# Cutting the first half of the tokens into two blocks of 512 columns instead of three, with the split inputs of both halves in one tile, spread side work and a later norm

## The chip, the cores and the metric

The kernel runs on one core of one Trainium2 chip. TensorE (PE) multiplies, VectorE (DVE), ScalarE (ACT) and GpSimd (POOL) do the elementwise work, and SyncE (SP) issues the DMAs. The metric is the device time of one execution in microseconds. Before the change three runs took 2689.2, 2690.6 and 2692.82 us; the median is 2690.6 us.

## What is computed

The reference is one inference step of one layer over 2048 prompt tokens and 64 sample tokens (8 sequences of 8), with 1024 model columns:

```python
mod = einsum('bd,de->be', silu(c), w_ada) + b_ada
sh1, sc1, g1, sh2, sc2, g2 = split(mod, 6)
h = rmsnorm(x, norm_mix_w) * (1 + sc1) + sh1
proj = einsum('bld,de->ble', h, w_in)
o_dn  = gated_deltanet(silu(conv4(qkv)), z, b, a)   # q, k normalised per head; 4 heads of 128
o_swa = sliding_window_attention(sq, sk, sv)        # 8 q heads, 2 kv heads, window 128
x = x + g1 * einsum('ble,ed->bld', concat(o_dn, o_swa), w_out)
h = rmsnorm(x, norm_ffn_w) * (1 + sc2) + sh2
gate, up = split(conv3(einsum('bld,df->blf', h, w_up)) + conv_b, 2)
x = x + g2 * einsum('blf,fd->bld', silu(gate) * up, w_down)
y = rmsnorm(x, final_norm_w)
```

The output also holds the new states of the convolutions, of the DeltaNet and of the attention cache. The arithmetic is float32.

## The kernel before

**Products.** Activations lie with the model columns on the partitions and the tokens along the free dimension. A projection is worked out one output row group of 128 columns (m) and one block of tokens (bi) at a time. Weights and inputs are split into a high and a low part that the faster float32 matmul takes, and each product is made of three: high by high, high by low and low by high (`gemm_steps`, L319). So one m on one block takes 8 (k) times 3 matmuls, all into one PSUM bank. The input projection has 22 m, the output projection 8, the up projection 44.

**Halves and blocks.** The tokens are cut into two halves, and each half into three blocks: `HALVES = [[(0, 384), (384, 384), (768, 256)], [(1024, 384), (1408, 384), (1792, 320)]]` (L36). The second half's up projection is mostly done with a cheaper scheme of its own (`up_quarters`), and the down projection has its own blocks of 512; neither is touched, apart from one norm.

**Order of the work.** Python generators lay the work out. `beside(steps, filler, share)` (L334) takes one step of side work and then so many steps (three matmuls each) of a projection as filler; `rest` runs what is left of the filler. `lockstep` runs several generators a step at a time in turn, `chain` one after the other. The framework then orders the instructions of each engine by that order and its own timing estimates, so an instruction can stand somewhat earlier on its engine than the Python text says; each engine runs its own list in order. All DMAs are issued by SP.

The stages, with their times in the profile:

1. 0 to 82 us: the inputs and the first modulation weights (w_ada, comps 0 and 1) are loaded; as each of eight k of the modulation comes, `affine_h` makes the split input h of the blocks for that k and the first two m of the input projection take it (`first_two`, steered by `PLAN`).
2. 82 to about 262 us: m 2 to 11 of the first half as filler beside the tasks: the rest of the modulation (`ada_cols`), the sums of down weights (`weight_sums`), the bias tables, the gates and the norm of the second half's tokens (`x_rstd`). `SHARE[3]` = 8.
3. 262 to 360 us: m 12 to 21 beside the first chunks of the DeltaNet (`ahead`).
4. 360 to 820 us: the second half's input projection beside the DeltaNet and attention of the first half (`mixers`). When the first half's h block is read for the last time, `freed` calls `second`, which makes the second half's h in the place.
5. 820 to 950 us: `between(0)`: the output projection of the first half (`outproj`, weights by `out_weights`), its norm and the next h (`ffn_in`).
6. 917 to 1612 us: the first half's up projection, beside the second half's mixers and the sample work (950 to 1478 us); then `between(1)`, the second half's up projection in two schemes (to 2206 us), and the down projection in two passes of seven products with the last norm (`down_phase`).

**Evacuation.** `conv_block` (L515) takes a PSUM bank: ACT copies it into a buffer and starts the convolution, DVE adds the other taps, three in the input projection and two in the up projection (L531). `silu2` (L542) makes twice the SiLU out of a Tanh (ACT, L545) and one more DVE instruction (L546); the factor two is taken out later, in `front`.

**Where h lies.** Each block has its own high and low tile, `hi0`, `lo0`, `hi1` and so on, and its own tile for the factors of the norm (`sg0`, `sg1`, `sg2`).

Of the kernel before, what the change touches and what calls it, by code (L numbers as in the profile page):

```python
# [14 lines left out]
F32 = mybir.dt.float32  # L15
# [7 lines left out]
P = 128  # L23
D = 1024
KT = 8
# [10 lines left out]
HALVES = [[(0, 384), (384, 384), (768, 256)], [(1024, 384), (1408, 384), (1792, 320)]]  # L36
# [58 lines left out]
def kernel(  # L95
# [69 lines left out]
    def ada_load(comp, kt, wpool, wt=None):  # L165
        if wt is None:
            wt = wpool.tile([P, KT, P], F32, tag="wada", name="wada", bufs=4)
        loads.append(nc.sync.dma_start(wt, I["w_ada"][KT * comp + kt]).ins)
        return wt
# [99 lines left out]
    def x_rstd(hf, bi, rB, pool, bank):  # L269

        c0, n = HALVES[hf][bi]
        acc = pool.tile([P, HB[0]], F32, tag="xacc", name="xacc", bufs=2)[:, :n]
        for k in range(KT):
            x = pool.tile([P, HB[0]], F32, tag="xst", name="xst", bufs=5)[:, :n]
# [7 lines left out]
        yield from token_rstd([acc], n, rB, pool, bank)  # L282

    def first_rstd(bi, xs, rB, pool, bank, eng):
# [3 lines left out]
        for k in range(KT):  # L288
            t = pool.tile([P, HB[0]], F32, tag="xst", name="xst", bufs=XST)[:, :n]
# [11 lines left out]
    def rB_tile(bi):  # L301
        return gw.tile([P, HB[bi]], F32, tag=f"sg{bi}", name=f"rB{bi}")

# [53 lines left out]
    def project(ms, src, load, hb, hf, evac, after=None, freed=None, tags=("acc",), turn=(2, 2), third=None, w0=None):  # L357


        order = list(pairs(ms, turn))  # L360
# [5 lines left out]
        for i, (m, bi) in enumerate(order):  # L366
            ps = bank(src, tags[i % len(tags)])
            yield from gemm_steps(ps, w[m], hb[bi], HALVES[hf][bi][1])
            if bi == 2 and new:
                w[new[0]] = load(new[0])  # L370
                new.pop(0)
            evac(m, bi, ps)
            if bi == 2 and after:
                after(m)
# [7 lines left out]
    def pairs(ms, turn):  # L382
# [4 lines left out]
        for g in [ms[:a]] + [[m] for m in ms[a:b]] + [ms[b:]]:  # L387
            for bi in range(3):
                for m in g:
                    yield m, bi  # L390
# [124 lines left out]
    def conv_block(ps, n, np_, hist, state, w, bias, dst):  # L515
# [3 lines left out]
        rb = evp[0].tile([P, 3 + HB[0]], F32, tag="rb", name="rb", bufs=evp[1])  # L519
# [20 lines left out]
        return rb  # L540

# [29 lines left out]
    def in_evac(hf, bi, m, ps, ic):  # L571
# [20 lines left out]
    def inproj(hf, h, ic, ms, **kw):  # L592
        return project(ms, "in_ps", lambda m: load_split(I["w_inT"][m], nc.gpsimd if m % 2 else nc.vector), h, hf,
# [28 lines left out]
    def front(c, d, pool, rows=P):  # L622
# [17 lines left out]
        for i in range(2):  # L640
# [7 lines left out]
            yield True  # L648

        nc.vector.tensor_scalar_add(ss[:rows], ss[:rows], 4 * EPS)  # L650
# [16 lines left out]
        nc.vector.tensor_scalar_mul(nr[:rows, :, 0], nr[:rows, :, 0], 0.5)  # L667
# [461 lines left out]
    def mix_tiles(op):  # L1129
        return [[op.tile([P, KT, HB[bi]], F32R, tag=f"{t}{bi}", name=t) for t in ("mixh", "mixl")] for bi in range(3)]  # L1130

    def mix_load(hf, bi, mix, op):
        c0, n = HALVES[hf][bi]
        hi, lo = mix[bi]
        for k in range(KT):
            if bi < 2:
                tag, bufs = (("xr", 2), ("acc", 3))[k % 2]
                t = op.tile([P, HB[0]], F32, tag=tag, name="mt", bufs=bufs)[:, :n]
# [11 lines left out]
    def out_weights():  # L1150

        seq = [m for o in OUT_ORDER for m in o]
# [10 lines left out]
    def outproj(hf, bi, mix, sums, op, weights, kept=None):  # L1163
# [3 lines left out]
        if kept is not None:  # L1167
            x2 = op.tile([P, KT, HB[0]], F32, tag="mixh0", name="x2")
            kept += [[x2[:, m] for m in range(KT)], op.tile([P, KT, LS], F32, tag="mixl0", name="x2s")]
        sums[bi] = op.tile([P, HB[0]], F32, tag="acc", name="acc", bufs=3)  # L1170
        c0, n = HALVES[hf][bi]
        np_ = n - LS if c0 + n == LT else n
        for i, m in enumerate(OUT_ORDER[bi]):
# [3 lines left out]
            xr = kept[0][m] if kept else op.tile([P, HB[0]], F32, tag="xr", name="xr", bufs=2)  # L1177
# [18 lines left out]
    def between(hf, filler, es, ms):  # L1196
# [3 lines left out]
        mix, sums = mix_tiles(op), {}  # L1200
        beside(chain(mix_load(hf, 0, mix, op), mix_load(hf, 1, mix, op)), filler, SHARE[4])
        rest(filler)
        weights = out_weights()
        steps = outproj(hf, 0, mix, sums, op, weights)
        beside(mix_load(hf, 2, mix, op), steps, 2)
        rest(steps)
        h = [h_tile(bi) for bi in range(3)]
# [927 lines left out]
```

## Time and profile before

| what | value |
| --- | --- |
| median of three runs | 2690.6 us |
| the profiled execution: own time, span of its instructions | 2689.79 us, 2688.0 us |
| PE busy | 2606.4 us, 97% of the span |
| weight loads (PEld, beside PE) busy | 2403.3 us, 89% |
| DVE, ACT, POOL busy | 1899.5, 1305.9, 788.2 us |
| mean granted PE clock | 0.99 |
| DMA | 438.07 MB, 163 GB/s over the span |

A view by windows gives the busy time of each engine in a stretch of time, the granted clock of PE (1.00 is full) and the rate of the DMAs. A view of groups gives, for one line, engine, operation and shape, how many there were, their busy time in us and the mean of one in ns, and what ended the idle time before them. The timeline gives single instructions: start and length in us, and in brackets how long the engine idled before, and for whom. Matmuls overlap in the pipeline, so the length of one is longer than the time it adds; the distance between the starts of neighbours is what counts. PE busy at 97% is for the same reason not PE at its peak.

### The profile page before, as it was taken

Reading aid. Unit: us, or ns where it says so; the run is one execution under the profiler, and the core shown is the slowest. Engines: PE = TensorE matmul, PEld = TensorE weight load, DVE = VectorE, ACT = ScalarE, POOL = GpSimd, SP = SyncE. Lnnn points to the kernel's source line nnn. Section 1 sums busy time; section 2 is a strip of 40 time slices with the busy share of each in tenths; the row PEclk is TensorE's granted clock in tenths of the full one; section 3 lists DMA queues with packets and bytes.
Section 4 is the critical chain, followed back from the end, with each engine's and each line's share of the span. In section 5 each row is a group of like instructions: output and inputs, shape, how many; then the busy total and the mean of one; then the engine's idle time right before and its main releaser. Section 6 shows DMA issues by size and latency. Waiting matters only on the chain.

```text
span 2688.0 us, 50078 instructions
## 1 busy us (share of the span) xinstructions
PE 2606.4 (97%) x18344; PEld 2403.3 (89%) x18344; DVE 1899.5 (71%) x3933; ACT 1305.9 (49%) x3404; POOL 788.2 (29%) x682
## 2 busy tenths in 40 slices
PE   7998999999999999999999999999999999999998
PEld 5898988788999998888898899999999997879988
DVE  7667579888523778898868565786776666676676
ACT  6444255555233555455553454555555554444343
POOL 2024243343222412222211113345555520020022
PEclk9999989999999999999999999999999999999999
DMA  7677444232256542333245337324555458677673
GB/s 281 229 266 247 123 144 117 78 96 83 92 146 202 178 141 78 96 99 88 74 155 186 117 111 253 130 82 156 171 168 174 172 181 297 213 248 246 224 244 131
DMA packets 318660, 438.07 MB, mean 163 GB/s; under 512 B 83107, under 2 KB 221572, under 8 KB 318148
## 3 DMA queue, kind: packets, MB, share of 16 engines
q1 hardware_dynamic: 318412, 434.85, 49.6%
q8 instruction: 144, 2.36, 0.4%
q14 instruction: 104, 0.85, 0.1%
HBM read 320.44 MB, written 115.33 MB: 162 GB/s over the span
## 4 chain that ended last, share of the span: by engine, by line
PE 57%; DMA 5%; DVE 4%; issue 2%; POOL 2%; ACT 1%; SPq 0%; POOLq 0%; DVEq 0%; ACTq 0%
PE up_ps L324 20%; PE dn_ps L1751 13%; PE op_ps L324 5%; PE uq_b L1541 4%; PE uq_c L1541 2%; PE in_ps L324 2%; PE uq_g L1541 2%; PE uq_u L1541 2%; DMA tr<-T_d 1%; DMA rawu<-in_w_upT_dram 1%; PE uq_a L1541 1%; PE pv_ps L971 1%; DMA rawg<-in_w_upT_dram 1%; PE as_ps L934 1%; DVE w_lo L316 1%
## 5 line engine op out<-in xcount | busy, mean ns | idle before, releaser
L324 PE MATMUL up_ps<-hi,w_hi 128*128 128x384 f32 (+2 forms) x1152 | 377.0, 327 | 0.0
L324 PE MATMUL up_ps<-hi,w_lo 128*128 128x384 f32 (+2 forms) x1152 | 370.4, 322 | 0.6 <-DVE w_lo L316 0.6
L324 PE MATMUL up_ps<-lo,w_hi 128*128 128x384 f32 (+2 forms) x1152 | 370.7, 322 | 0.0
L324 PE MATMUL in_ps<-hi,w_hi 128*128 128x384 f32 (+2 forms) x1056 | 346.7, 333 | 3.8 <-ACT hi L265 1.1
L324 PE MATMUL in_ps<-lo,w_hi 128*128 128x384 f32 (+2 forms) x1056 | 347.6, 330 | 2.2 <-DVE lo L266 1.3
L324 PE MATMUL in_ps<-hi,w_lo 128*128 128x384 f32 (+2 forms) x1056 | 346.8, 329 | 1.3 <-POOL w_lo L316 1.3
L1751 PE MATMUL dn_ps<-th,wh 128*128 128x512 f32 (+2 forms) x796 | 273.1, 344 | 4.9 <-DVE x L1219 4.0
L1751 PE MATMUL dn_ps<-tl,wh 128*128 128x512 f32 (+2 forms) x796 | 273.2, 343 | 3.6 <-DVE tl L1643 3.6
L1751 PE MATMUL dn_ps<-th,wl 128*128 128x512 f32 (+2 forms) x796 | 272.3, 344 | 0.0
L324 PEld LDWEIGHTS up_ps<-hi,w_hi 128*128 128x128 f32 x1152 | 217.4, 189 | 15.9 <-issue 10.2
L324 PEld LDWEIGHTS up_ps<-lo,w_hi 128*128 128x128 f32 x1152 | 217.5, 189 | 8.6 <-issue 7.3
L324 PEld LDWEIGHTS up_ps<-hi,w_lo 128*128 128x128 f32 x1152 | 217.3, 189 | 8.7 <-issue 6.4
L324 PEld LDWEIGHTS in_ps<-hi,w_hi 128*128 128x128 f32 x1056 | 199.7, 190 | 18.2 <-issue 10.2
L324 PEld LDWEIGHTS in_ps<-lo,w_hi 128*128 128x128 f32 x1056 | 201.0, 190 | 11.0 <-issue 4.5
L324 PEld LDWEIGHTS in_ps<-hi,w_lo 128*128 128x128 f32 x1056 | 201.0, 190 | 8.3 <-issue 4.9
L316 DVE TENSOR_TENSOR w_lo<-w_raw,w_hi 128x1024 fp32r<-128x1024 f32 x111 | 140.7, 1268 | 83.2 <-ACT w_hi L315 82.2
L315 ACT CAST w_hi<-w_raw 128x1024 fp32r<-128x1024 f32 x132 | 138.0, 1046 | 119.6 <-PE in_ps L324 39.2
L531 DVE SCALAR_TENSOR_TENSOR ev<-rb,cw,ev 128x384 f32<-128x384 f32 (+1 forms) x216 | 147.3, 688 | 34.0 <-ACT ev L524 31.4
L1751 PEld LDWEIGHTS dn_ps<-th,wh 128*128 128x128 f32 x796 | 151.7, 191 | 21.9 <-ACT wh L1642 2.5
L1751 PEld LDWEIGHTS dn_ps<-tl,wh 128*128 128x128 f32 x796 | 151.6, 190 | 19.7 <-DVE tl L1643 3.9
L1751 PEld LDWEIGHTS dn_ps<-th,wl 128*128 128x128 f32 x796 | 151.4, 190 | 15.7
L1642 ACT CAST wh<-wr 128x512 fp32r<-128x512 f32 x149 | 92.1, 618 | 149.4 <-PE dn_ps L1751 119.6
(545 smaller groups left out, 6728.2 us busy)
## 6 DMA issues: line engine op xcount, KB each, us to landing
w_raw<-in_w_upT_dram SPq DMA_DIRECT2D x50, 512.0 KB
wada<-in_w_ada_dram SPq DMA_DIRECT2D x44, 512.0 KB
w_raw<-in_w_inT_dram SPq DMA_DIRECT2D x44, 512.0 KB
wr<-ws_d SPq DMA_DIRECT2D x88, 256.0 KB
w_raw<-in_w_outT_dram SPq DMA_DIRECT2D x40, 512.0 KB
proj<-ev SPq DMA_DIRECT2D x88, 192.0 KB
d<-act_d SPq DMA_DIRECT2D x33, 512.0 KB
wr<-in_w_downT_dram SPq DMA_DIRECT2D x66, 256.0 KB
```

Of the source, the lines that this page charges most:

```text
L315: nc.scalar.copy(hi, raw)
L316: (eng or nc.vector).tensor_tensor(lo, raw, hi.bitcast(F32), ALU.subtract)
L324: nc.tensor.matmul(ps[:, :n], a[:, k, :], b[:, k, :n], start=first is not False and k == ks[0] and i == 0, stop=last is not False and k == ...
L531: nc.vector.scalar_tensor_tensor(out, src(j), w[:, j:j + 1], out, ALU.mult, ALU.add)
L934: nc.tensor.matmul(banks[v][:, 256 * g + P * k0:256 * g + 256], a[r, g0 + g], b[r, keys], start=i == 0, stop=i == 2, tile_position=(64 * v ...
L971: nc.tensor.matmul(pv_ps[64 * v:64 * v + 64, :], (vprev[0], vt)[half][:, 64 * v:64 * v + 64], PT[v, half], start=half == k0, stop=half == 1)
L1541: nc.tensor.matmul(bk[t][:, :nb], u[:, k], v[:, k], start=new and k == 0 and y == 0, stop=k == KG - 1 and y == 2, skip_group_check=True)
L1642: nc.scalar.copy(h, raw)
L1751: nc.tensor.matmul(acc[m, s][:, :n], w[q, i][a][:, c], th[b][:, v], start=new and i == 0 and y == 0, stop=i == KH - 1 and y == 2, skip_gro ...
```

## The change

1. The first half has two blocks of 512. Loops over `range(3)` become loops over the number of blocks. The second half keeps its three.
2. One tile for the high and one for the low part (`h_at`), of 8 times 1088 columns; `h_tile(hf, bi)` gives a block's slice of it. The norm's factors (`sg_at`) likewise. A block of the second half no longer lies exactly where a block of the first half lay, so `second` makes h in two goes: block 0 and a quarter of block 1 when the first block is free, the rest when the second is.
3. In the first half's input projection SiLU is ACT's own function (`TWICE`), without the DVE instruction; DVE makes all low parts of weights there, where POOL made those of odd m.
4. Side work is spread: `spaced` adds empty steps, and the shares fall accordingly: `SHARE[3]` from 8 to 2.05, `SHARE[0]` from 8 to 5.4, `SHARE[2]` from 6 to 4, and others. At the start, `PLAN` is that of two blocks, the modulation weights have six buffers of their own (before: four, and four more in tiles of h), and the first load of x is 512 columns.
5. In the first pass of the down projection the norm of group 2 starts one product later (after j = 5 instead of j = 4), as it does in the second pass.

```diff
-HALVES = [[(0, 384), (384, 384), (768, 256)], [(1024, 384), (1408, 384), (1792, 320)]]
+HALVES = [[(0, 512), (512, 512)], [(1024, 384), (1408, 384), (1792, 320)]]
+NX = HALVES[1][0][1]
...
-    def h_tile(bi):
-        return [slot.tile([P, KT, HB[bi]], F32R, tag=f"{t}{bi}", name=f"{t}{bi}") for t in ("hi", "lo")]
+    h_at = []
+
+    def h_tile(hf, bi):
+
+        c0, n = HALVES[hf][bi]
+        a = KT * (c0 - HALVES[hf][0][0])
+        return [t[:, a:a + KT * n].rearrange("p (k n) -> p k n", k=KT) for t in h_at]
...
-        yield from token_rstd([acc], n, rB, pool, bank)
+        yield from spaced(token_rstd([acc], n, rB, pool, bank))
+
+    def spaced(steps, n=4):
+
+        for _ in steps:
+            for _ in range(n):
+                yield True
...
-            silu2(ev, rb)
+            if TWICE[hf] == 2:
+                silu2(ev, rb)
+            else:
+                nc.scalar.activation(ev, ev, AF.Silu)
...
-        return project(ms, "in_ps", lambda m: load_split(I["w_inT"][m], nc.gpsimd if m % 2 else nc.vector), h, hf,
+        return project(ms, "in_ps", lambda m: load_split(I["w_inT"][m], nc.gpsimd if hf and m % 2 else nc.vector), h, hf,
...
-        for bi in range(2):
-            steps = outproj(hf, bi + 1, mix, sums, op, weights, kept if bi else None)
+        for bi in range(nb - 1):
+            steps = outproj(hf, bi + 1, mix, sums, op, weights, kept if bi + 2 == nb else None)
             beside(ffn_in(hf, bi, h, sums, op), steps, SHARE[5])
             rest(steps)
         up = up_proj(hf, h, uc[0], op, ms)
-        beside(ffn_in(hf, 2, h, sums, op, *kept), up, SHARE[6])
+        beside(ffn_in(hf, nb - 1, h, sums, op, *kept), up, SHARE[6][hf])
...
-            if j == 4 and not ip:
-                finish = norm(2, 0, PW, x, sums[2], cols[2], free[4:6], wait=2)
-            elif j == 4:
+            if j == 4:
                 late = (2, 0, PW, x, sums[2], cols[2])
-            elif j == 5 and ip:
-                finish = norm(*late, free[-2:])
+            elif j == 5:
+                finish = norm(*late, free[-2:], wait=2 - ip)
...
-    PLAN = [(3, 1), (3, 1), (3, 1, 2), (3, 4, 4, 2), (3, 4, 4, 2), (3, 4, 5, 5), (3, 4, 5, 5), (3, 4, 5)]
-    HB = (384, 384, 320)
-    SHARE = (8.0, 2.0, 6.0, 8.0, 2.0, 5.0, 2.0, 8.0)
+    XST, WADA = 6, 6
+    PLAN = [(2,), (2, 1), (2, 1), (2, 1, 3), (2, 3, 3), (2, 3), (2, 3, 3), (2, 3)]
+
+    SHARE = (5.4, 2.0, 4.0, 2.05, (2.0, 1.4), 5.0, (1.3, 2.0), 8.0)
...
         tasks = lockstep(
-            chain(*[ada_cols([(c, k + q) for q in range(4)], ac, st, at_bank) for c in range(2, 6) for k in (0, 4)],
-                  weight_sums(range(6), sa)),
+            chain(*[spaced(ada_cols([(c, k + q) for q in range(4)], ac, st, at_bank), 2) for c in range(2, 6) for k in (0, 4)],
+                  spaced(weight_sums(range(6), sa), 2)),
...
-            for _ in range(28):
+            for _ in range(20):
                 next(filler)
...
-        def second(bi):
-            h1.append(h_tile(bi))
-            rest(affine_h(h1[bi], bi, 1, 0, rBs[bi], I["xT"]))
+        def second(freed):
+
+            if not freed:
+                h1[:] = [h_tile(1, bi) for bi in range(3)]
+            for bi, ks in (((0, range(KT)), (1, range(KT // 4))), ((1, range(KT // 4, KT)), (2, range(KT))))[freed]:
+                rest(affine_h(h1[bi], bi, 1, 0, rBs[bi], I["xT"], ks))
```

More of the change, by code (lines that the diff above doesn't have):

```diff
@@ L368, in project @@
             yield from gemm_steps(ps, w[m], hb[bi], HALVES[hf][bi][1])
-            if bi == 2 and new:
+            end = bi == len(HALVES[hf]) - 1
+            if end and new:
                 w[new[0]] = load(new[0])
@@ L372, in project @@
             evac(m, bi, ps)
-            if bi == 2 and after:
+            if end and after:
                 after(m)
@@ L1290, in token_quarters @@
         for t in ("T2", "T3", "T1", "T4"):
-            q[t] = [pool.tile([P, KG, HB[0]], F32R, tag=f"{t}{s}", name=t) for s in "hl"]
+            q[t] = [pool.tile([P, KG, NX], F32R, tag=f"{t}{s}", name=t) for s in "hl"]
         return q
```

118 lines of the change are left out of this document (61 added, 57 removed).

## The prediction

> **What bounds the kernel now.** I read the stages by windows first, to see which engine each waits for (columns: PE, weight loads, DVE, ACT, POOL busy us, granted clock, DMA share, GB/s).
>
> ```profile
> 820.00:917.00 97.00, 94.59 (x602) 93.69 (x601) 56.45 (x78) 44.53 (x74) 39.30 (x32) 1.00 0.71 233
> 950.00:1478.00 528.00, 522.46 (x4379) 466.39 (x4378) 432.72 (x1179) 272.87 (x930) 123.78 (x87) 1.00 0.38 116
> 1478.00:1612.00 134.00, 134.00 (x816) 125.86 (x815) 83.47 (x135) 65.52 (x182) 17.84 (x13) 1.00 0.33 114
> 2206.00:2688.00 482.00, 458.90 (x2590) 408.22 (x2588) 324.66 (x532) 209.97 (x389) 64.89 (x51) 0.98 0.69 228
> ```
>
> PE is never long idle; beside the mixers (950 to 1478) DVE comes nearest, 433 of 528 us. The chain that ended last agrees: its long pieces are matmuls without a break.
>
> ```profile
> 776.76 43.53 PE in_ps L324 x264
> 820.29 41.16 PE op_ps L324 x233
> 1534.22 77.89 PE up_ps L324 x500
> ```
>
> So the pace of the matmuls is the first question, then the few places where PE stands. For the pace I take the distance of starts in the timeline: one m of the up projection on blocks of 384, 384 and 256, and a run of 512-column matmuls of the down projection.
>
> ```profile
> 1567.16 0.34 PE L324 MATMUL up_ps<-hi,w_hi 128*128 128x384 f32 x1
> 1575.49 0.28 PE L324 MATMUL up_ps<-hi,w_hi 128*128 128x256 f32 x1
> 1578.36 0.34 PE L324 MATMUL up_ps<-hi,w_hi 128*128 128x384 f32 x1
> 2289.66 0.39 PE L1751 MATMUL dn_ps<-th,wh 128*128 128x512 f32 x1
> 2311.87 0.39 PE L1751 MATMUL dn_ps<-th,wl 128*128 128x512 f32 x1
> ```
>
> From 1567.16, 48 matmuls of 384 take 8.33 us, 173.5 ns each; the next 24 of 256 take 2.87 us, 119.6 ns each; 98 of 512 (first to last start) take 22.21 us, 226.6 ns each. Between 256 and 512 a column costs 0.418 ns, and 119.6 less 256 of those leaves about 13 ns per matmul whatever its width. That is what fewer, wider matmuls save.
>
> **The change, part by part.** The sum is made against the profiled execution, 2689.8 us (span 2688.0), 0.8 us under the median of 2690.6.
>
> (a) Pace. Three matmuls (2 x 173.5 + 119.6 = 466.6 ns) become two (453.2 ns): 13.4 ns. This happens for every m, k and product of the first half: (22 + 8 + 44) x 8 x 3 = 1776 times, 23.8 us. The rows of 256 columns carry that count (one of three products):
>
> ```profile
> L324 PE MATMUL up_ps<-hi,w_hi 128*128 128x256 f32 x344 | 99.2, 288 | 0.0
> L324 PE MATMUL in_ps<-hi,w_hi 128*128 128x256 f32 x176 | 49.0, 286 | 0.4 <-ACT hi L262 0.4
> L324 PE MATMUL op_ps<-mixh,w_hi 128*128 128x256 f32 x64 | 18.1, 282 | 0.0
> ```
>
> 344 + 176 + 64 is 584; the other eight use the third weight's own tiles. The first two m run in the start-up, where PE waits anyway, so I count 72 m: -23.
>
> The Trainium skill, page "TensorE: Matmul & The Clock Gate", section "Back-to-back issue gap", gives an isolated gap of N/2.4 + 2.5 ns, that is 162.5, 109.2 and 215.8 ns. By it the three cost 434.2 and the two 431.7 ns, and 1776 times 2.5 ns is an estimate of 4.4 us. The trace does not agree: its distances are 10 to 11 ns higher.
>
> (b) Spread side work. Between 82 and 262 us the tasks make 37 joint steps (8 bias tables, 11 of gates, 18 of norms) and ask for 8 x 37 = 296 filler steps, but 10 m x 3 x 8 - 28 = 212 are there: the last ten or so have no matmuls beside them.
>
> ```profile
> 214.37 0.44 PE L324 MATMUL in_ps<-hi,w_lo 128*128 128x384 f32 x1 [1.32 <-POOL w_lo L316]
> 224.50 1.19 PE L222 MATMUL rb_ps<-dg,ones 128*128 128x128 f32 x4 [6.73 <-DVE dg L218]
> 226.54 0.79 PE L222 MATMUL rb_ps<-dg,ones 128*128 128x128 f32 x2 [0.53 <-DVE dg L218]
> 227.45 0.52 PE L324 MATMUL in_ps<-lo,w_hi 128*128 128x384 f32 x1
> 230.97 0.44 PE L324 MATMUL in_ps<-hi,w_hi 128*128 128x384 f32 x1
> 220.00:240.00 20.00, 14.97 (x81) 14.60 (x81) 18.66 (x30) 10.78 (x29) 9.99 (x9) 0.74 0.69 253
> ```
>
> PE stands 8.6 us for a norm whose turn came too early, and the granted clock then falls: 11 distances from 227.45 to 230.97 take 320 ns instead of 173.5, 1.6 us more. After the change the tasks make 68 steps (spread modulation 32, sums 36) and ask for 2.05 x 68 = 139 of 10 x 2 x 8 - 20 = 140: filler for all of them, and no w_lo on POOL. Of 10.2 us I take 8. Next late is the sums' DMA and DVE work, which must end before the DeltaNet's pool opens; but m 12 to 21 do not need that pool.
>
> (c) Output projection. 192 (m, k, product) times 466.6 ns are 89.6 of 97 us. In the 256 block a weight must come every 24 x 119.6 = 2.9 us, and PE waits for it:
>
> ```profile
> 907.71 0.38 PE L324 MATMUL op_ps<-mixh,w_lo 128*128 128x256 f32 x1 [1.40 <-DVE w_lo L316]
> ```
>
> With 512 it is every 5.4 us. Of 7.4 us I take 2; the norms around it stay.
>
> (d) Later norm, first pass of the down projection.
>
> ```profile
> 2376.10 1.05 PE L214 MATMUL dn_ps<-ones,dsum 128*128 128x1 f32 x8 [0.83 <-POOL dsum L1231]
> 2387.65 1.41 PE L222 MATMUL dn_ps<-dg,ones 128*128 128x128 f32 x8 [3.58 <-DVE dg L218]
> 2550.00:2600.00 50.00, 50.00 (x231) 41.81 (x230) 35.93 (x49) 24.00 (x42) 10.73 (x8) 1.00 0.76 251
> ```
>
> The norm's two kinds of matmul stop PE for 4.4 us in the sixth product, the one that loads two tiles for each input. In the second pass, where that norm already starts after the product, the same stretch runs without a stop (last row). I take -4 (0, if the stop only comes a product later, to -6, with a slow clock behind it). The norm's y stores move past one product's loads on SP, and the seventh product has one load for each input.
>
> (e) DVE and ACT. The taps' rows give the fixed part:
>
> ```profile
> L531 DVE SCALAR_TENSOR_TENSOR rB<-rb,fcw,rB 128x384 f32<-128x384 f32 x100 | 68.1, 683 | 28.0 <-ACT rB L526 26.7
> L531 DVE SCALAR_TENSOR_TENSOR rB<-rb,fcw,rB 128x256 f32<-128x256 f32 x50 | 26.1, 521 | 2.1 <-ACT rB L526 1.7
> L316 DVE TENSOR_TENSOR w_lo<-w_raw,w_hi 128x1024 fp32r<-128x1024 f32 x111 | 140.7, 1268 | 83.2 <-ACT w_hi L315 82.2
> L546 DVE SCALAR_TENSOR_TENSOR ev<-rb,ev 128x384 f32<-128x384 f32 x48 | 31.1, 649 | 8.4 <-ACT rb L545 8.0
> 30.58 1.28 ACT L438 ACT_TABLE_LOAD   x1
> ```
>
> 128 columns more cost 0.16 us, so 512 take about 0.85 (an estimate) and one tap of one m falls from 1.89 to 1.69 us. Over 44 m with three DVE instructions each that is 26 us of DVE; since PE is busy nearly all of that stretch I take -2 (bounds 0 and -6). In the input projection 12 m lose the SiLU instruction (2 x 0.65 + about 0.5 us each, 21 us) and DVE takes 11 low parts from POOL (14 us): nothing, because DVE has room there. ACT's own SiLU beside the gates' Exp and Ln means other tables; with at most six more loads of 1.28 us, beside matmuls with several banks in hand, +0.5.
>
> (f) What gets tighter, and the shares.
>
> ```profile
> L259 DVE SCALAR_TENSOR_TENSOR ht<-ht,MOD,rB 128x384 f32<-128x384 f32 x16 | 11.5, 752 | 2.4 <-DMA ht<-in_xT_dram 2.4
> L266 DVE SCALAR_TENSOR_TENSOR lo<-ht,MOD,hi 128x384 fp32r<-128x384 f32 x32 | 27.8, 877 | 1.2 <-ACT hi L265 1.2
> 10.00:20.00 10.00, 7.32 (x68) 6.14 (x71) 5.79 (x18) 3.34 (x6) 1.87 (x1) 1.00 1.03 397
> 140.00:160.00 20.00, 20.00 (x174) 17.57 (x174) 12.93 (x28) 7.75 (x22) 2.38 (x1) 1.00 0.81 290
> ```
>
> `second`: one k of h costs DVE 0.75 us, and 0.88 more for even k, 1.2 us on average. Ten k in the first go are 12 us, while the cover (m 20 and 21 on the last block) falls from 48 x (173.5 + 119.6) ns = 14.1 to 48 x 226.6 = 10.9 us. The next matmuls take h k by k, so +1 (0 to 12, all of it bare). `ffn_in` before the up projection: three m on one block, 72 x 226.6 ns = 16.3 us, instead of on two, 144 x 173.5 = 25.0 us, cover the norm and 8 k of 512 columns, twelve DVE instructions of 0.85 = 10 us, beside three evacuations: +2 (0 to 8). The third weight's tiles are now those of the last block and free only when the output projection ends: +0.5. Start: 0.5 MB more before the first squares, at 397 GB/s 1.3 us, and modulation weights fetched six tiles ahead instead of eight, while the bytes that fill the DMA there stay the same in all: +1 (-2 to +4). The side work of 82 to 262 us asks for its bytes in less time, where a good 20 us moved 290 GB/s: +2 (0 to 11). The other shares fall with the filler's steps: beside one step of the second half's mixers lie 4 x 3 x 226.6 ns = 2.7 us instead of 6 x 3 x 155.5 = 2.8, nothing.
>
> Sum: -23 - 8 - 2 - 4 - 2 + 0.5 + 1 + 2 + 0.5 + 1 + 2 = -32, from 2689.8 to 2657.8; with the 0.8 us to the median, 2658.6 us.
>
> **The rivals.** Rows for the first two:
>
> ```profile
> 50.53 0.29 DVE L195 TENSOR_REDUCE MOD<-adat_ps 128x9 f32<-128x36 f32 x2
> 49.57 1.41 ACT L261 ACTIVATE ht<-ht,MOD 128x384 f32<-128x384 f32 x3
> L1751 PE MATMUL dn_ps<-th,wh 128*128 128x256 f32 x244 | 68.9, 283 | 0.2 <-DVE x L1219 0.2
> ```
>
> *One tile, one order (slower).* If writes into one slice of the shared h wait for matmuls on another slice, and later matmuls for the writes, covers vanish at three places. `second`: 24 k of 1.2 us, 29 us. `ffn_in` beside the up projection, in both halves: 8 k each at DVE 0.75, ACT 0.5 (three in 1.41 us) and DVE 0.88 in a row, 17 us each. Together 63 us against the 32 gained: 2721. It decides from the point where half of those covers is lost. Against it: MOD is one tile too, and there DVE starts to write one k at 50.53 while ACT still reads others, from 49.57 to 50.98.
>
> *Width gives little.* The 226.6 ns are from the down projection, whose tiles lie differently. If a 512-column matmul takes 232 ns in this projection, the two cost 464 instead of 453 ns and (a) gives 4 us, not 23: 2677. Against it: at 256 columns, which both have, a matmul's length in the trace is 283 ns there and 288 in the row of up_ps in (a).
>
> The gap formula of the Trainium skill, in the section named in (a), would lead to about this time.
>
> *DMA takes the spread back.*
>
> ```profile
> 82.00:176.00 94.00, 91.22 (x951) 77.94 (x947) 49.40 (x105) 40.01 (x110) 4.80 (x3) 1.00 0.77 272
> 176.00:262.00 86.00, 77.20 (x489) 75.86 (x489) 70.06 (x111) 43.49 (x118) 42.29 (x37) 0.94 0.71 247
> ```
>
> If these bytes come no faster than before, the 8 us of (b) and 10 m of the pace (10 x 24 x 13.4 ns = 3.2 us) are lost: 2669. For it: the DMA engines' share is 0.71 to 0.77 over all of the stage. Against: 397 GB/s at 10 to 20 us.
>
> *Tighter covers fail.* `second` and `ffn_in` at their upper bounds, 20 - 3 = 17 us, and the slow clock after each, 1.6 us: 2679.
>
> **How the numbers follow.** Forecast 0.60; better than forecast, with several terms at their good bounds, 0.05; width 0.06; DMA 0.14; covers 0.10; one order 0.05. The likeliest gives 2658. All good bounds together ((b) -10, (c) -7, (d) -6, (e) -6, nothing for (f) but -2 at the start) would be 2636, the low end; the high end, 2683, is the covers' rival with half of the 9 us that the DMA's bound still holds. About 0.15 is left out. A measurement of this kernel can tell 0.2%, 5.4 us. Slower takes the 0.05 and 0.01 for mishaps together; same 0.06, where two of the other rivals meet (2677 and 2669 come to 2688); faster the rest, 0.88.
>
> **What would show it.** After the change: starts of in_ps, op_ps and up_ps of 512 columns 227 ns apart; no stop over 2 us between 200 and 240 us and a clock of 1.00 there; no rb stop in the first pass's sixth product; the up projection of the first half about 14 us shorter. Wrong would be: 512-column starts over 230 ns, new stops at the first matmuls on the second half's h or the second block of the up projection, waits of ada_ps for wada, or a tail in which the sums hold the DeltaNet back.

## The result, and the profile after

The kernel after takes 2659.8 us (median of four runs, 2657.6 to 2662.2) where the one before, in four runs, took 2691.7. The ratio is 0.9877 with a 95% interval of 0.9854 to 0.9900: 33 us faster (27 to 39). The forecast was 2658. The total came out. The parts did not all come out, and that is what the experiments are about.

The profiled execution took 2661.34 us (span 2659.2). First the pace: the starts of one run of up_ps matmuls in the timeline of the kernel after (start and length in us).

```profile
1560.17 0.39 PE L340 MATMUL up_ps<-hi,w_lo 128*128 128x512 f32 x1
...
1572.41 0.39 PE L340 MATMUL up_ps<-hi,w_lo 128*128 128x512 f32 x1
```

From the first to the last start lie 54 distances, 12.24 us, 226.7 ns each: the forecast's figure. Then the stretch where the side work was spread, by windows (PE, weight loads, DVE, ACT, POOL busy us, granted clock, DMA share, GB/s), and the one stop of PE in it, from the timeline.

```profile
200.00:220.00 20.00, 20.00 (x93) 16.63 (x92) 11.32 (x18) 9.45 (x23) 0.53 (x1) 1.00 0.68 233
220.00:240.00 20.00, 16.11 (x72) 13.00 (x70) 13.97 (x19) 5.80 (x13) 0.00 (x0) 0.98 0.67 226
240.00:260.00 20.00, 19.22 (x81) 15.81 (x81) 10.28 (x22) 8.30 (x24) 10.64 (x12) 0.85 0.81 257
```

```profile
240.78 0.79 PE L340 MATMUL in_ps<-hi,w_hi 128*128 128x512 f32 x1 [4.67 <-DVE ev L604]
```

The stop of 6.73 us at an rb_ps matmul is gone, but a new one of 4.67 us stands 16 us later, and the clock falls to 0.85 behind it. It waits for a bank whose evacuation is queued on DVE behind this:

```profile
232.74 0.69 DVE L1621 TENSOR_TENSOR suv<-suv 128x512 f32<-128x512 f32 x1 [2.73 <-DMA suv<-in_w_downT_dram]
```

DVE, which runs its list in order, stood 2.73 us for the load of the weight sums. A second new stop is at the start of the up projection (timeline of PE, then of ACT):

```profile
927.57 0.79 PE L340 MATMUL up_ps<-hi,w_hi 128*128 128x512 f32 x1 [7.34 <-ACT cv L543]
928.16 0.63 PE L340 MATMUL up_ps<-lo,w_hi 128*128 128x512 f32 x1
928.58 0.63 PE L340 MATMUL up_ps<-hi,w_lo 128*128 128x512 f32 x1
...
931.57 0.62 PE L340 MATMUL up_ps<-hi,w_hi 128*128 128x512 f32 x1
```

```profile
918.71 0.73 ACT L271 ACTIVATE hi<-ht,MOD 128x512 fp32r<-128x512 f32 x1 [4.13 <-DVE ht L265]
...
926.13 0.72 ACT L267 ACTIVATE ht<-ht,MOD 128x512 f32<-128x512 f32 x1
926.75 0.76 ACT L543 ACTIVATE cv<-up_ps,fcb,fcw 128x512 f32<-128x512 f32 x1
```

`between(0)` leaves room for only some 15 filler steps; then the tags of the banks are narrowed to the two of `acc`. The fourth bank of the up projection is therefore the second one again, and its evacuation (926.75) sits in ACT's list behind the making of the next h. PE stands 7.34 us, and the next matmuls start 427 ns apart, which is 2 us more: 9.3 in all.

The later norm's two matmuls in the first pass of the down projection carry no wait any more:

```profile
2379.44 0.95 PE L215 MATMUL dn_ps<-ones,dsum 128*128 128x1 f32 x8
...
2386.70 1.05 PE L223 MATMUL dn_ps<-dg,ones 128*128 128x128 f32 x8
```

For what follows I cut every profiled execution into stages by the first start of a group of matmuls in the timeline: to the first as_ps (attention begins), to the second half's first ba_ps, to the first op_ps, to the first up_ps, to the second half's op_ps, to the first dn_ps, to the last dn_ps. In us, with the ratio of all runs to the kernel before:

| kernel | to as_ps | to ba_ps | to op_ps | op | up | to dn_ps | down | ratio |
| --- | --- | --- | --- | --- | --- | --- | --- | --- |
| before | 362.5 | 87.2 | 370.4 | 96.9 | 694.9 | 594.3 | 474.5 | 1 |
| after | 355.4 | 83.9 | 371.0 | 91.4 | 690.0 | 592.9 | 467.5 | 0.9877 |
| a_lsum (the same program) | 356.7 | 82.2 | 371.0 | 91.4 | 689.6 | 595.3 | 468.6 | 0.9883 |
| a_three | 356.7 | 76.6 | 378.9 | 92.7 | 708.1 | 593.5 | 467.5 | 0.9966 |
| a_clump | 351.9 | 83.9 | 369.8 | 91.4 | 691.1 | 592.9 | 466.7 | 0.9878 |
| a_banks | 355.2 | 77.3 | 372.7 | 91.4 | 691.0 | 594.6 | 466.3 | 0.9879 |
| a_lowpool | 357.2 | 84.7 | 382.1 | 91.4 | 691.0 | 595.0 | 466.5 | 0.9930 |
| a_old_e | 363.9 | 85.1 | 380.1 | 91.4 | 693.5 | 593.9 | 470.0 | 0.9972 |
| a_pool | 356.4 | 109.8 | 366.7 | 91.4 | 692.6 | 594.1 | 468.7 | 0.9965 |
| a_dve2 | 354.9 | 84.1 | 356.9 | 91.4 | 690.6 | 594.7 | 469.6 | 0.9855 |
| b_late | 364.6 | 89.5 | 371.4 | 97.2 | 695.6 | 593.9 | 465.9 | 0.9975 |
| b_spread | 367.5 | 87.2 | 369.8 | 98.3 | 693.0 | 592.6 | 473.8 | 1.0008 |
| b_silu | 352.9 | 102.2 | 374.7 | 98.5 | 693.8 | 595.3 | 477.4 | 1.0042 |
| b_rest | 356.4 | 88.4 | 363.3 | 99.3 | 694.2 | 593.6 | 469.2 | 0.9919 |

Labels with a_ start from the kernel after, those with b_ from the one before. Two columns need care. a_banks has the instructions of the kernel after in the same order up to the up projection, and yet its stage to ba_ps took 77.3 us instead of 83.9: a single execution says little in that stage. And the first ba_ps does not always stand at the same place of PE's list: 528 matmuls lie in that stage in the kernel after, 680 in a_pool, 588 in the kernel before and 731 in b_silu. So the two stages from the first as_ps to the first op_ps are best taken together; with the order of the kernel after they took 454.9, 453.2 (a_lsum) and 450.0 us (a_banks).

### The profile page after: what moved, and what is told of

It is laid out like the page before. It is cut to its first block, busy times and chain, and to the rows that moved or that the text cites. A ratio compares the mean times of both kernels' runs of the same rounds, so it can differ in the third digit from the quotient of the medians.

```text
span 2659.2 us, 45647 instructions
## 1 busy us (share of the span) xinstructions
PE 2583.2 (97%) x16552; PEld 2231.5 (84%) x16552; DVE 1828.3 (69%) x3681; ACT 1262.5 (47%) x3081; POOL 752.7 (28%) x643
## 5 line engine op out<-in xcount | busy, mean ns | idle before, releaser
L340 PE MATMUL in_ps<-hi,w_hi 128*128 128x512 f32 (+2 forms) x880 | 317.6, 364 | 9.5 <-DVE ev L604 4.7
L340 PE MATMUL up_ps<-hi,w_hi 128*128 128x512 f32 (+2 forms) x808 | 316.4, 392 | 7.3 <-ACT cv L543 7.3
L340 PE MATMUL in_ps<-lo,w_hi 128*128 128x512 f32 (+2 forms) x880 | 318.4, 362 | 2.7 <-DVE lo L272 1.7
L340 PE MATMUL in_ps<-hi,w_lo 128*128 128x512 f32 (+2 forms) x880 | 315.9, 359 | 0.0
L340 PE MATMUL up_ps<-lo,w_hi 128*128 128x512 f32 (+2 forms) x808 | 312.9, 387 | 0.0
L340 PE MATMUL up_ps<-hi,w_lo 128*128 128x512 f32 (+2 forms) x808 | 311.7, 387 | 0.0
L340 PEld LDWEIGHTS up_ps<-hi,w_hi 128*128 128x128 f32 x808 | 152.3, 188 | 46.3 <-issue 11.4
L340 PEld LDWEIGHTS in_ps<-lo,w_hi 128*128 128x128 f32 x880 | 167.1, 190 | 26.6 <-issue 7.6
L340 PEld LDWEIGHTS up_ps<-lo,w_hi 128*128 128x128 f32 x808 | 152.4, 189 | 33.2 <-issue 8.5
L340 PEld LDWEIGHTS up_ps<-hi,w_lo 128*128 128x128 f32 x808 | 152.3, 189 | 30.6 <-issue 4.0
L548 DVE SCALAR_TENSOR_TENSOR ev<-rb,cw,ev 128x512 f32<-128x512 f32 (+2 forms) x180 | 131.4, 734 | 26.9 <-ACT ev L541 25.1
```

Of the source, the lines that this page charges most:

```text
L340: nc.tensor.matmul(ps[:, :n], a[:, k, :], b[:, k, :n], start=first is not False and k == ks[0] and i == 0, stop=last is not False and k == ...
L548: nc.vector.scalar_tensor_tensor(out, src(j), w[:, j:j + 1], out, ALU.mult, ALU.add)
```

## The experiments

**a_three: the width alone undone.**

```diff
-                nc.tensor.matmul(ps[:, :n], a[:, k, :], b[:, k, :n], ...)
+                for c in (slice(0, cut), slice(cut, n)) if cut else (slice(0, n),):
+                    nc.tensor.matmul(ps[:, c], a[:, k, :], b[:, k, c], ...)
...
+            yield from gemm_steps(..., cut=256 if not hf and bi else None)
```

> The kernel after, but wherever the first half's second block of 512 is multiplied (input projection from m 2 on, output projection, up projection), each matmul of 512 columns is issued as two of 256 into the same bank, so per k and product there are three matmuls again for 1024 columns; blocks, evacuations, tiles, DMAs and order stay. Theory 'pace' (fewer, wider matmuls are the main gain): 226.6 + 2 x 119.6 = 465.8 ns in place of 453.2, 12.6 ns, times (20 + 8 + 44) x 24 = 1728, is 21.8 us, so about 2682 us (2677 to 2686). Rival 'side work' (the gain comes from spread tasks, the later norm and less DVE and ACT work, and PE waits anyway for most of what it would save): 0 to 6 us, 2660 to 2666.

Measured: 0.9966 (0.9952 to 0.9980) against 0.9877 for the kernel after, so 0.0089 of 2691 us, 24 us. The price can also be read directly in its timeline; each x2 row is one pair of 256 columns.

```profile
1584.77 0.40 PE L341 MATMUL up_ps<-hi,w_hi 128*128 128x256 f32 x2
...
1590.52 0.40 PE L341 MATMUL up_ps<-hi,w_hi 128*128 128x512 f32 x1
```

24 pairs take 5.75 us, 239.6 ns each, where one matmul of 512 takes 226.7: 13 ns for one instruction more. The loss lies mostly where these matmuls are, 18.1 us in the up projection. 'Pace' holds here, and 'side work', which expected 0 to 6 us, falls. (The framework also orders the other instructions differently here, so the 24 us have an error beyond their interval; the 13 ns have not.)

**b_rest, b_spread, b_silu, b_late: the rest of the change, whole and in parts, on the kernel before.**

```diff
# b_spread
-        yield from token_rstd([acc], n, rB, pool, bank)
+        yield from spaced(token_rstd([acc], n, rB, pool, bank))
...
-    SHARE = (8.0, 2.0, 6.0, 8.0, ...
+    SHARE = (8.0, 2.0, 6.0, 3.1, ...
# b_silu
-            silu2(ev, rb)
+            if hf:
+                silu2(ev, rb)
+            else:
+                nc.scalar.activation(ev, ev, AF.Silu)
...
-    load_split(I["w_inT"][m], nc.gpsimd if m % 2 else nc.vector)
+    load_split(I["w_inT"][m], nc.gpsimd if hf and m % 2 else nc.vector)
# b_late
-            if j == 4 and not ip:
-                finish = norm(2, 0, PW, x, sums[2], cols[2], free[4:6], wait=2)
...
+            if j == 4:
                 late = (2, 0, PW, x, sums[2], cols[2])
```

> The kernel before, three blocks in the first half as they were, with all of the change that does not need the two blocks: the spread tasks (share 3.1 in place of 8, since three blocks give 212 filler steps for 68 joint steps), ACT's own SiLU and all low parts on DVE in the first half's input projection, and the norm of group 2 a product later. Theory 'pace': the sum of these terms, -8 - 4 + 0.5 and a little for DVE, that is 10 to 14 us, about 2678 us (2674 to 2682). Rival 'side work': most of the 31 us, 2660 to 2666.

Measured: 0.9919 (0.9906 to 0.9932), 22 us faster. That lies between the two theories, 8 us more than 'pace' allowed for; together with the 24 us of the width it is more than the whole gain, 46 against 33. Reckoned from this kernel to the kernel after (0.9919 to 0.9877), the width is worth only 11 us. One difference can be named: a_three keeps the two blocks and with them the stop at the start of the up projection (7.35 us in its timeline), so its 24 us do not carry what the blocks cost.

> The kernel before with the tasks of 82 to 262 us spread alone (share 3.1 in place of 8). The kernel before with everything but the width ran at 0.9919, 22 us less, where the terms of the prediction for it sum to about 13. Theory 'the terms hold, each a little larger': 8 to 11 us from the spread, ratio 0.996 to 0.997, and the stop of 6.73 us at rb_ps (224.5 us) gone. Rival 'given back': with two blocks, undoing the spread cost nothing (0.9878 against 0.9877), so it gains 0 to 4 us here too, ratio 0.9985 to 1, the stop moved to the stage's end.

Measured: 1.0008 (0.9999 to 1.0016): nothing. Its timeline of PE shows why:

```profile
200.81 0.68 PE L222 MATMUL rb_ps<-dg,ones 128*128 128x128 f32 x4 [2.19 <-DVE dg L218]
...
252.05 0.58 PE L330 MATMUL in_ps<-hi,w_hi 128*128 128x256 f32 x1 [5.09 <-DVE ev L587]
```

The stop of 6.73 us has become 2.19, and a stop of 5.09 us, an evacuation behind DVE's list, has come 51 us after it. 2.19 and 5.09 are more than the 6.73 they replace. 'Given back' holds.

> The kernel before with ACT's own SiLU and all low parts of weights on DVE in the first half's input projection, and nothing else. Prediction: about -1.5 us, ratio 0.999 to 1. Rival 'POOL was the late one': the low parts made by POOL (one PE stop of 1.32 us behind a w_lo of POOL at 214 us) and the SiLU instructions hold the stage's side work, and without them the part of b_rest that the other terms do not explain, 6 to 10 us, comes from here: ratio 0.9965 to 0.998.

Measured: 1.0042 (1.0030 to 1.0054), 11 us slower, outside both theories. The table shows two things in one kernel: attention begins 9.6 us earlier than before, and the two stages behind lose 15 and 4 us. The timeline of those stages has these stops among others:

```profile
367.85 0.47 PE L938 MATMUL as_ps<-kh,qh 64*128 64x128 f32 x1 [4.52 <-DVE nl L948]
...
563.50 0.68 PE L759 MATMUL z_ps<-T,AM 64*64 64x64 f32 x8 [2.64 <-DVE T L799]
...
610.34 1.08 PE L665 MATMUL d_ps<-gm,tgtr 128*128 128x512 f32 x2 [4.20 <-ACT junk L650]
```

None of these instructions was edited; of the mixers' only one small DVE instruction for each chunk in `front` is left out, the factor two. They stand in another order, though: the framework lays the lists out anew. That this order is the cause is not shown.

> The kernel before with the norm of group 2 one product later in the down projection's first pass, and nothing else. Theory of the prediction: the stops of 0.83 and 3.58 us in the sixth product go, 4 us; by the down phase of the kernel after (7.0 us shorter) up to 7: ratio 0.9974 to 0.9985. Rival 'the stop comes a product later': ratio 1.000.

Measured: 0.9975 (0.9965 to 0.9986), 6.7 us. All but the down projection keeps its order here (in the two traces some 50 of PE's 18,344 matmuls stand elsewhere in the list), so this is a clean price. The sixth product, by windows, before and then in b_late:

```profile
2350.00:2400.00 50.00, 45.59 (x201) 37.34 (x200) 38.67 (x54) 19.80 (x35) 13.59 (x9) 0.97 0.72 232
```

```profile
2350.00:2400.00 50.00, 50.00 (x223) 41.41 (x222) 35.70 (x52) 21.74 (x39) 5.50 (x4) 1.00 0.76 247
```

PE goes from 45.59 to 50.00 us busy of 50: the 4.4 us of the two stops. The granted clock goes from 0.97 to 1.00 there as well. The rest of the 6.7 is not traced.

The three parts alone sum to 2 + 11 - 7, 6 us slower; together they are 22 us faster. They do not add, and the table shows where: from the first as_ps to the first op_ps the three alone sum to 22 us more, of which b_silu has 19.3, and b_rest takes 5.9 us less there. In all other stages they sum to 9 us less, and b_rest has 10.4. So the difference lies in stages that hardly any of the edits touches.

**a_clump: the spread undone in the kernel after.**

```diff
     def spaced(steps, n=4):
-        for _ in steps:
-            for _ in range(n):
-                yield True
+        yield from steps
...
-    SHARE = (5.4, 2.0, 4.0, 2.05, ...
+    SHARE = (5.4, 2.0, 4.0, 5.3, ...
```

> The kernel after with the tasks of 82 to 262 us not spread (37 joint steps, share 5.3, which is 8 x 140 / 212). Theory 'the norms came too early for their matmuls': the last ten joint steps have no filler beside them again, a stop of some 7 us at an rb_ps matmul and a slow granted clock behind it come back, 8 to 10 us: 2668 to 2670. Rival 'the spread only moved the wait' (the new stop of 4.67 us at an in_ps matmul at 240.8 us, behind the tasks' weight sums on DVE, takes its place): 0 to 4 us, 2660 to 2664, with that stop gone or smaller.

Measured: 0.9878 (0.9864 to 0.9892), the same time. The stop at rb_ps comes back, with 3.71 us, and the one of 4.67 us is gone:

```profile
209.91 1.20 PE L223 MATMUL rb_ps<-dg,ones 128*128 128x128 f32 x4 [3.71 <-DVE dg L219]
```

So the spread is worth nothing with two blocks either; 'only moved the wait' holds.

**a_lsum: weight sums later in their unit.**

```diff
-                  spaced(weight_sums(range(6), sa), 2)),
+                  spaced(weight_sums(range(6), sa), (4, 1, 1))),
```

> The kernel after with the six steps of each unit of weight sums cut as 4 (load), 1 (sums), 1 (stores) instead of 2, 2, 2, so that DVE comes to the sums later after their loads are issued. Theory: the stop of 4.67 us at in_ps (240.8 us) is made by DVE standing 2.73 us for the suv load with an evacuation queued behind it; it goes, and with the slow clock behind it 4 to 6 us: ratio 0.9855 to 0.9865. Rival 'given back': the stage from 350 to 440 us, where DVE is busy 38 of 40 us, sets when the mixers go on, and the ratio stays at 0.9877 (0.987 to 0.9885) though the stop is gone.

Measured: 0.9883 (0.9868 to 0.9898). The framework made the same instructions in the same order out of it on every engine, so it is the kernel after, timed once more, and the theory stayed untested. It is useful as a measure: two timings of one program differ by 0.0006, while the stop at 240 us, 4.67 us in one execution, is 6.24 in the other.

**a_banks: six banks for the start of the up projection.**

```diff
             filler, _ = between(0, in_end(), es, range(MU))
+            for _ in range(34):
+                next(filler)
             up_tags[:] = ["acc"]
```

> The kernel after, but the first six banks of the first half's up projection are taken from all six free banks: 34 more filler steps are run before the tags are narrowed to the two banks of acc. Theory 'bank': the stop of 7.34 us at 927.6 us is the fourth up_ps bank, which waits for the evacuation of the second one behind the ACT instructions of the next h; with six banks the stop and the ten matmuls at half the pace behind it go: 7 to 9 us less, 2651 to 2653. Rival 'the work for h itself is late': PE stops at the first matmul on the second block's h instead, for the same time, 2658 to 2660.

Measured: 0.9879 (0.9866 to 0.9893), the same time. 'Bank' was right about the cause of the stop and wrong about its price: with more banks the stop is gone (windows of a_banks),

```profile
910.00:930.00 20.00, 18.89 (x87) 15.26 (x86) 14.87 (x18) 10.22 (x19) 9.27 (x9) 1.00 0.04 14
```

with PE busy 18.89 of 20 us there, but the stage is not shorter (691.0 against 690.0). The 34 filler steps are missing later, and the mixers' work beside the filler comes in another order. Groups of PE from 900 to 1612 us, the same 64 matmuls in the kernel after and in a_banks, and a stop in a_banks:

```profile
L959 PE MATMUL as_ps<-kh,qh 64*128 64x256 f32 x64 | 15.4, 334 | 0.0
```

```profile
L959 PE MATMUL as_ps<-kh,qh 64*128 64x256 f32 x64 | 17.9, 334 | 0.0
```

```profile
1447.13 1.94 PE L1042 MATMUL pot_ps<-PO,pc 128*64 128x512 f32 x2 [4.46 <-issue]
```

Each matmul is as long as before (334 ns), but they overlap less, so together they are busy longer; all three as_ps groups together go from 41.1 to 48.5 us.

**a_old_e, a_lowpool, a_pool, a_dve2: who makes the low parts.**

```diff
# a_lowpool (a_old_e: this, and TWICE = (2, 2))
-    load_split(I["w_inT"][m], nc.gpsimd if hf and m % 2 else nc.vector)
+    load_split(I["w_inT"][m], nc.gpsimd if m % 2 else nc.vector)
# a_pool
-    rest(affine_h(h1[bi], bi, 1, 0, rBs[bi], I["xT"], ks))
+    rest(affine_h(h1[bi], bi, 1, 0, rBs[bi], I["xT"], ks, pool_too=lambda k: True))
# a_dve2
-    load_split(I["w_inT"][m], nc.gpsimd if hf and m % 2 else nc.vector)
+    load_split(I["w_inT"][m], nc.vector)
```

> The kernel after with both edits of the first half's input projection undone: SiLU as Tanh and a DVE instruction again, and the low parts of odd m on POOL. Alone, the spread was worth nothing (1.0008), the later norm 6.7 us (0.9975) and these edits even cost 11 us (1.0042), but all three together gained 22 (0.9919). Theory 'one bundle': DVE's and POOL's relief only pays where the tasks are spread, and the spread only with the relief; so 8 to 17 us are lost here: ratio 0.991 to 0.994. Rival, the prediction's term (e): 0 to 2 us, 0.9877 to 0.9885.

Measured: 0.9972 (0.9960 to 0.9985), 26 us slower than the kernel after, more than the theory had. 8.5 us of it come before attention begins (363.9 against 355.4), 9 in the stage to op_ps. PE stands 24.8 us from the first as_ps to the first op_ps, where it stands 16.4 in the kernel after.

> The kernel after with the low parts of odd m in the first half's input projection on POOL again, ACT's own SiLU kept. Theory 'low parts': a weight split on POOL takes 2.4 us instead of DVE's 1.27 and comes late for its matmuls, so most of what the run with both edits undone loses is lost here, 5 to 12 us, ratio 0.9895 to 0.992. Rival 'SiLU': the DVE instructions carry it, and this run stays at 0.987 to 0.9885.

Measured: 0.9930 (0.9913 to 0.9946), 14 us. The loss is rather more than 'low parts' said, and not where it said: up to attention only 1.8 us are lost, and 11.1 in the stage to op_ps, where no weight split was edited. Stops there:

```profile
476.27 0.92 PE L780 MATMUL u_ps<-inv,Y 64*64 64x64 f32 x8 [2.39 <-DVE Y L828]
...
522.84 0.38 PE L959 MATMUL as_ps<-kh,qh 64*128 64x256 f32 x1 [2.65 <-ACT vt L944]
```

> The kernel after with all low parts of the second half's h (the work of the two goes of second) on POOL, where DVE made those of even k: some 12 DVE instructions of 0.6 us leave the stretch of 350 to 440 us, where DVE is busy 38 of 40 us, and POOL takes them at 1.18 us each, of which it has room. Theory 'DVE sets that stretch, and gains made ahead of it are lost there': 5 to 9 us less, ratio 0.9843 to 0.986. Rival 'the chain of the mixers' own instructions sets it': 0.987 to 0.9885, or slower if POOL's queue holds the mixers.

Measured: 0.9965 (0.9954 to 0.9977), 24 us slower. The theory's gain did not come; of the rival only the "or slower" did. 355 to 440 us by windows in the kernel after and in a_pool:

```profile
355.00:440.00 85.00, 76.80 (x539) 68.45 (x537) 75.53 (x200) 50.74 (x176) 34.13 (x28) 0.86 0.38 114
```

```profile
355.00:440.00 85.00, 75.27 (x491) 64.12 (x492) 70.10 (x175) 50.60 (x170) 46.26 (x39) 0.78 0.35 105
```

In these 85 us POOL does 12 us more and DVE 5 us less, but PE gets through fewer matmuls too, at a clock of 0.78. For equal work, take the whole stretch from the first as_ps to the first op_ps, again in the kernel after and in a_pool:

```profile
355.40:810.30 454.90, 438.53 (x3441) 385.50 (x3441) 330.36 (x918) 216.64 (x714) 158.26 (x132) 0.97 0.36 106
```

```profile
356.40:832.90 476.50, 458.50 (x3442) 401.89 (x3442) 328.92 (x909) 221.08 (x723) 165.54 (x142) 0.94 0.35 101
```

It takes 21.6 us longer. DVE's busy time hardly falls (330.4 to 328.9 us), so the relief that the theory counted on did not come, and what DVE's busy time costs there stays open. PE stands 18.0 us in place of 16.4, and only one of its stops ends on POOL (0.4 us). Nearly all of the loss is 20.0 us more of busy time for the same matmuls, at a granted clock of 0.94 in place of 0.97. Why the clock is lower is not shown.

> The kernel after with all low parts of weights on DVE in the second half's input projection too, where POOL still makes those of odd m (11 of 2.4 us each; DVE takes 1.3 to 1.5). Moving low parts the other way cost 14 us (0.993, weights of the first half) and 24 us (0.9965, h of the second half), all of it after 355 us. Theory 'POOL's queue': PE's stops of 350 to 820 us that end on POOL's PT and o (0.92, 0.48 and 0.55 us) and those behind them get shorter when POOL has 27 us less to do, 3 to 8 us, ratio 0.985 to 0.9866. Rival 'another order': an edit there makes the framework lay out the instructions behind it anew (2801 lines of PE's order differ), and the time of 355 to 820 us moves by that, either way: then the ratio lies outside, above 0.988, or the gain has nothing to do with stops on POOL.

Measured: 0.9855 (0.9839 to 0.9872), 2651.15 us, the fastest of all. It is 6 us faster than the kernel after (0.9877) and 7 faster than the same program in a_lsum (0.9883), but the intervals overlap, so this gain is small against the noise. 440 to 810 us by windows, in the kernel after and in a_dve2:

```profile
440.00:810.00 370.00, 361.83 (x2906) 316.98 (x2905) 255.23 (x720) 166.21 (x540) 124.13 (x105) 1.00 0.36 105
```

```profile
440.00:810.00 370.00, 367.89 (x2860) 324.87 (x2861) 255.28 (x716) 165.20 (x523) 97.73 (x91) 1.00 0.38 111
```

POOL has 26 us less, DVE no more than before, PE stands 2.1 us in place of 8.2. The stage to op_ps is 14.1 us shorter, and the stops on POOL that the kernel after has there are gone:

```profile
447.80 1.07 PE L996 MATMUL pv_ps<-PT,vt 128*64 128x512 f32 x2 [0.92 <-POOL PT L991]
...
608.84 1.08 PE L996 MATMUL pv_ps<-PT,vt 128*64 128x512 f32 x4 [0.55 <-POOL PT L991]
```

The ratio is inside the range of 'POOL's queue', at its good end. Three moves of low parts in the kernel after went the same way: onto POOL 14 and 24 us slower, off it 6 us faster. A fourth did not: b_silu took low parts off POOL in the kernel before, together with the SiLU instruction, and lost 11 us. How much of each is the order that the framework lays out anew is not separated: about 1500 of PE's 16,552 matmuls stand elsewhere in a_dve2's list, and the stops that went sum to less than the 14 us.

## Why the prediction was right, point by point

By its own stages, against the profiled executions (before 2689.79, after 2661.34, so -28.4):

| stage | its terms | measured |
| --- | --- | --- |
| start to attention | (a) 20 m -6.4, (b) -8, start +1, DMA +2, table loads +0.5: -11 | -7.1 |
| to op_ps | `second` +1 | -2.7 |
| output projection | (a) -2.6, (c) -2 | -5.5 |
| up projection | (a) -14.2, ffn_in +2, third +0.5, DVE -2 | -4.9 |
| to dn_ps | nothing | -1.4 |
| down projection | (d) -4 | -7.0 |

**(a) was right** in mechanism, and in size for each matmul. The mean distance between two up_ps starts in a row is 180.8, 180.8 and 124.0 ns before, twice 240.8 after. That is 485.6 against 481.6 ns; but the 9.3 us of the stop at 927 us are 9.5 ns of it (978 such pairs), so without that stop 13.5 ns are saved, where the forecast had 13.4. (By the medians, 174, 174 and 120 ns against twice 227, it is 14 ns. In a_banks, which does not have the stop, the mean is 238.3 ns, so 9 ns are saved.) What it is worth in the whole is less certain: 24 us when undone in the kernel after, 11 us when added to b_rest. So by the first reckoning the pace is the main gain, by the second the rest of the change is. The 215.8 ns that the forecast worked out from the Trainium skill's formula do not appear: the kernel after shows 226.7.

**(b) failed.** The step "Of 10.2 us I take 8" took the length of a stop for its price. The stop did go, as said, and another came, on an engine that the step did not look at: DVE, made to wait for the sums' loads with PE's evacuations queued behind. "Next late is the sums' DMA and DVE work" was right, the conclusion that nothing needs it in time was not. Alone it gained nothing, and undone it cost nothing.

**(e) failed the other way.** "Nothing, because DVE has room there" holds for DVE's busy time. But an engine that works through its list in order can be late in one place and still have room in the sum. Undoing that edit costs 26 us in the kernel after; done alone it brought attention forward by 9.6 us, and lost more behind. Which instruction carries the 26 us is not shown; the low parts alone carry 14 of them (a_lowpool). The stage to attention gained 7.1 us in all; with this edit undone it is 1.4 us longer than before the change, so that here the pace's 6.4 us cannot be seen at all, and the spread's 8 were never there.

**(c) and (d) were right and somewhat small**: 2.9 us in place of 2 for (c) (5.5 less the 2.6 of the pace, by the stage's time alone), 6.7 (3.8 to 9.4) in place of 4 for (d).

**(f):** The 1 us of `second` cannot be seen: its stages fell by 2.7 us, and executions with one order scatter by nearly 5 us there. The cover of ffn_in did fail, for 9.3 us, above the bound of 8, and not because the norm and the eight k are long, but because the narrower cover lets the narrowing of the banks come earlier. That is half of the rival 'tighter covers'. Yet removing the stop gained nothing (a_banks), so it is not 9.3 us of the total either. The start lost 3.2 us to the first in_ps, and had 2.9 of them back at the first toep_ps.

That the number was met so closely is in part luck. The pace was worked out rightly, but two errors, 8 us too much for (b) and too little for (e), lay on opposite sides, and the start and the up projection were wrong by 4 and 9 us. Of the signs that the forecast named, starts 227 ns apart and the vanished rb_ps stop in the sixth product came. No stop over 2 us between 200 and 240 us (it is 4.67), a clock of 1.00 there (0.98, and 0.85 behind) and an up projection 14 us shorter (it is 4.9) did not. Of the rivals, 'width gives little' falls by the 227 ns. 'One tile, one order' falls too: the longest stop of in_ps matmuls between 340 and 450 us, where the second half's h is made and first used, is 0.4 us.

**What stays open** is why times change where nothing was edited. From the beginning of attention to the first op_ps b_silu, a_lowpool and a_old_e lost 10 to 19 us, though nothing was edited there but one small DVE instruction for each chunk in two of them (the factor two of SiLU in `front`). Part of it can be seen: in a_lowpool and a_old_e PE stands 26.1 and 24.8 us there where it stands 16.4 in the kernel after, at the same clock of 0.97. In b_silu it stands 26.6 us where it stood 13.9, and the clock is 0.96 in place of 0.98. In a_dve2, which gained, it stands 12.2 us, at 0.99.

The framework lays out each engine's list by its own estimates, and an edit of a few instructions at 100 us changes over a thousand places behind it. That this order makes the difference is only argued, and one run speaks against it: a_clump edits nothing but the order of side work, by its trace about half of PE's 3441 matmuls in this stretch stand elsewhere in the list than in the kernel after (in a_dve2 and b_silu it is some 1500), and the stretch took 453.8 us against 454.9.

## What to carry to other kernels

Where PE's matmuls run back to back, count instructions: here each had a fixed 13 ns, and what the same columns save in fewer matmuls could be worked out beforehand. Charge apart what the wider blocks bring with them, here a stop of 7.34 us. The length of a stop that the profile shows is not its price: before removing it, look at who is queued behind the next engine that waits. And price a part both by undoing it in the finished kernel and by adding it to the old one. If the two disagree, as here, the parts do not add, and a total that was met does not show that its terms were right.

## What the runs showed of the hardware

Some DVE instructions take longer while POOL works. The timeline of DVE and of POOL in a_lowpool, where all gt and TU rows are about the same size:

```profile
515.38 0.21 DVE L733 TENSOR_TENSOR gt<-G,TU 32x60 f32<-32x60 f32 x1
515.62 0.21 DVE L735 TENSOR_TENSOR TU<-TU,gt 32x60 f32<-32x60 f32 x1
515.86 0.94 DVE L733 TENSOR_TENSOR gt<-G,TU 32x63 f32<-32x63 f32 x1
516.84 1.22 DVE L735 TENSOR_TENSOR TU<-TU,gt 32x63 f32<-32x63 f32 x1
```

```profile
515.68 1.05 POOL L659 TENSOR_TENSOR gm<-cst,ghl 128x512 fp32r<-128x512 f32 x1
516.69 1.29 POOL L690 TENSOR_TENSOR Dc<-Dc,cst 128x512 f32<-128x512 f32 x1
```

An instruction of 0.21 us takes 0.94 and 1.22 us, and ends at 516.80 and 518.06 us, each within 0.1 us of the end of POOL's instruction (516.73 and 517.98). The Trainium skill, page "SBUF — State Buffer", section "SBUF: two separate sides", says that a POOL instruction that reads SBUF and a DVE instruction with two SBUF inputs share a pair of ports as an exclusive lock, held for the whole instruction. The trace agrees: the DVE instruction is held until POOL's ends. A size that fits this is in a_dve2: from the first as_ps to the first op_ps DVE makes 22 low parts of weights there instead of 11, 13.9 us more, while POOL's busy time falls from 158.3 to 134.0 us; DVE's busy time rises by only 2.3 us, from 330.4 to 332.6. It is a reason to keep low parts off POOL that the forecast did not weigh, though these runs do not price it in the kernel's time.
